# A rotary embedding over 16 heads: the first piece of the first tile loaded in two halves of 64 partitions, ahead of the tables

## The chip, the cores and the metric

The kernel runs on one core of a Trainium2 chip. The metric is the device time of one execution in microseconds; the time given for a kernel is the median of its runs. A core has five engines (TensorE, VectorE, ScalarE, GpSimd, SyncE) with a queue of instructions each, and 16 DMA engines that move the data. A DMA is issued by an instruction on an engine's queue (here SyncE's and ScalarE's), and its packets then wait in a ring that belongs to that queue, one on each DMA engine.

## The reference

```
batch, seq, dim = x.shape            # 16, 512, 1024, float32
x = x.reshape(batch, seq, 16, 64)    # 16 heads of 64
x1, x2 = x[..., :32], x[..., 32:]
cos, sin: (512, 32), the same for every batch and head
out = concatenate([x1 * cos - x2 * sin, x1 * sin + x2 * cos], axis=-1)
```

Every element is read once and written once: 33.6 MB in and 33.6 MB out.

## The kernel before

**Tiles.** One tile holds two batches: 128 partitions, 64 for each batch (PB), and on each partition KK = 8 consecutive rows of 1024 elements, 32 KB. There are NT = 8 tiles of 4 MB and BUFS = 5 buffers for them, so tiles 0 to 4 are loaded at once and tiles 5 to 7 when the stores of tiles 0 to 2 have landed. Tiles are changed in place and stored from the same buffer.

**Loads and stores.** `load` (L70) and `store` (L76) each issue one DMA for the rows lo to hi of a tile. Before the change the order is this: SyncE issues the sin table (L83, 64 partitions of 1 KB), ScalarE the first piece of tile 0, rows 0 to 2 (L84; FIRST = (3, 8)), SyncE the cos table (L85), ScalarE the second piece, rows 3 to 7 (L87), and SyncE tiles 1 to 4 (L89). Then SyncE issues four tiny DMAs, `spare` (L92; EXTRA gives their numbers of rows). Stores are issued by SyncE, a whole tile at a time, only the last tile in two pieces of four rows (LAST_OUT, L193). After the third store SyncE issues the loads of tiles 5 to 7 (L198).

**Semaphores of the DMAs.** All DMAs that are issued by SyncE and ScalarE share eight semaphores in turn, in program order. So the ninth DMA waits, before it is issued, for the first to land, and so on: the spares wait for the tables and the pieces of tile 0, and the stores of tiles 0 to 2 wait for earlier loads too.

**Tables.** sin and cos arrive on 64 partitions. TensorE spreads them to 128 by a matrix of zeros and ones (`spread`), sin at L113 and cos at L114, both into one PSUM tile `tab`. VectorE then makes the signed sin table `sns` in SBUF (L116, L117) and a copy for row 0 (L119). L116 is released by TensorE's last matmul at L114. Everything else waits for these.

**Arithmetic of one tile.** The order is written out by hand (`manual_schedule`). GpSimd multiplies the swapped rows by `sns` (`sin_product`, L165): rows 1 and 2, then row 3, rows 4 and 5, rows 6 and 7. VectorE multiplies by cos into PSUM (`cos_product`, L141) and adds the two for the row pairs (`pair_sum`, L189). For row 0 (L150) and row 3, TensorE adds by a matmul with the identity (`pe_add`, L176) and ScalarE copies the sum back (L209, L181). The first work of GpSimd on a tile needs rows 1 and 2; VectorE's needs row 0; row 3 comes second on GpSimd.

**The end.** The last tile's first store (rows 0 to 3) waits for ScalarE's last copy at L181; its second store for VectorE's last sum at L189. The execution ends when the second store has landed.

Of the kernel before, what the change touches and what calls it, by code (L numbers as in the profile page):

```python
# [21 lines left out]
FIRST = (3, 8)  # L22
LAST_OUT = (4, 8)

EXTRA = (2, 4, 5, 6)


@with_exitstack
def kernel(
# [13 lines left out]
    nc = tc.nc  # L43
    P = nc.NUM_PARTITIONS
# [4 lines left out]
    PB = P // NB  # L49
    KK = seq // PB  # L50
# [3 lines left out]
    x_v = x.rearrange("(t b) (p k) d -> t (b p) (k d)", b=NB, k=KK)  # L54
# [12 lines left out]

    tiles = [None] * NT

    def load(t, lo=0, hi=KK, queue=nc.sync):  # L70
        if tiles[t] is None:
            tiles[t] = xp.tile([P, F], FP32, name="xt")
        s = slice(lo * dim, hi * dim)
        queue.dma_start(out=tiles[t][:, s], in_=x_v[t][:, s])

    def store(t, lo=0, hi=KK):  # L76
        s = slice(lo * dim, hi * dim)
        nc.sync.dma_start(out=out_v[t][:, s], in_=tiles[t][:, s])

    tabs = bp.tile([P, 2 * dim], FP32, name="b")  # L80
    sin_sb = tabs[:PB, : KK * half]
    cos_sb = tabs[:PB, dim : dim + KK * half]
    nc.sync.dma_start(out=sin_sb, in_=sin_v)  # L83
    load(0, 0, FIRST[0], nc.scalar)  # L84
    nc.sync.dma_start(out=cos_sb, in_=cos_v)  # L85
    for lo, hi in zip(FIRST, FIRST[1:]):
        load(0, lo, hi, nc.scalar)  # L87
    for t in range(1, BUFS):
        load(t)  # L89
    spare = fixed.tile([16, len(EXTRA), 16], FP32)  # L90
    for i, n in enumerate(EXTRA):
        nc.sync.dma_start(out=spare[:n, i], in_=sin_v[:n, :16])  # L92
# [7 lines left out]
    for ps in (own_ps[:, :BANK], own_ps[:, BANK:], pe_ps):  # L100
# [9 lines left out]
        out=spread.rearrange("p (b q) -> p b q", b=NB),  # L110
        in_=bass.AP(tensor=eye.tensor, offset=eye.offset, ap=[eye.ap[0], [0, NB], [1, PB]]),
# [147 lines left out]
```

## Time and profile before

| | |
|---|---|
| median of 3 runs | 163.85 us (163.66 to 164.0) |
| the profiled execution's own time | 163.66 us |
| its span | 161.9 us, 443 instructions |
| VectorE, GpSimd busy | 136.2 us, 127.1 us |
| bytes moved by the DMAs | 67.25 MB, 415 GB/s over the span |
| first piece of tile 0 issued, SyncE's first DMA issued | 0.73 us, 0.73 us |
| table matmuls begin: sin, cos | 8.13 us, 12.26 us |
| GpSimd's first product begins | 14.36 us |
| last tile's first and second store issued | 149.85 us, 152.0 us |

The page gives busy times by engine, the DMA queues (q1 is SyncE's, q10 ScalarE's) with their share of the 16 DMA engines' time, and a chain of waits followed back from the last instruction. Stretches of the span can be asked for by themselves: each line then gives a window in us, its length, the busy time of TensorE, its weight loads, VectorE, ScalarE and GpSimd with counts, the granted clock, the share of the 16 DMA engines' time, and GB/s. A DMA share a little over 1 comes from packets that are counted where they begin. Besides, the trace keeps a record of each DMA packet: queue, begin, length and bytes. A packet here is the run of one partition, so a piece of three rows gives 128 packets of 12 KB, eight for each of the 16 DMA engines; a record does not name its engine, but each engine handles one packet after the other, so begins and ends chain up into 16 lanes.

### The profile page before, as it was taken

What the parts mean: (1) busy time and instruction counts of PE and PEld (TensorE: products, weight loads), DVE (VectorE), ACT (ScalarE), POOL (GpSimd) and SP (SyncE); (2) the same over time, 40 slices, a digit from 0 to 9 for tenths busy, and PEclk for the clock granted to TensorE, in tenths of its full rate; (3) what the DMA queues carried; (4) which work ended last, traced back from release to release, by engine and by line L of the source; (5) the groups of instructions that cost most, each with busy time, mean ns of one, the idle gap of its engine ahead of it and who ended that gap; (6) DMA issues with size and microseconds to landing.
All of it is one profiled execution on the core that took longest, in us unless ns stands there. A gap on an engine that the chain in (4) does not pass through costs nothing.

```text
span 161.9 us, 443 instructions
## 1 busy us (share of the span) xinstructions
PE 61.2 (38%) x71; PEld 19.1 (12%) x71; DVE 136.2 (84%) x85; ACT 18.7 (12%) x25; POOL 127.1 (79%) x38
## 2 busy tenths in 40 slices
PE   3023290507550575039311923093407540574000
PEld 0011130102110211012101310040003100210000
DVE  1006996999999999999999999999999999999500
ACT  0000231100310030102010121003100310031000
POOL 1004999999999999998899889988998999891000
PEclk9999999555865577555855595558555765567555
DMA  5999999999999999998999999999998998996796
GB/s 182 432 398 445 429 478 389 429 478 389 429 478 389 405 502 389 405 502 389 421 480 389 437 470 389 437 470 389 429 478 389 445 462 389 470 429 275 328 449 259
DMA packets 2787, 67.25 MB, mean 415 GB/s; under 512 B 354, under 2 KB 482, under 8 KB 482
## 3 DMA queue, kind: packets, MB, share of 16 engines
q1 hardware_dynamic: 2498, 63.05, 90.6%
q10 hardware_dynamic: 288, 4.19, 6.7%
q14 instruction: 1, 0.01, 0.0%
HBM read 33.69 MB, written 33.55 MB: 415 GB/s over the span
## 4 chain that ended last, share of the span: by engine, by line
DVE 68%; issue 13%; DMA 7%; POOL 5%; PE 1%; SPq 0%; DVEq 0%
DVE xt L189 33%; DVE pd L141 31%; DMA b<-in_cos_dram 7%; POOL b L165 5%; DVE pe_ps L141 3%; PE tab L114 1%; SPq L83 0%; DVE sns L116 0%; DVE xt L150 0%; DVE own_ps L141 0%; DVE sns L117 0%; DVEq L189 0%
## 5 line engine op out<-in xcount | busy, mean ns | idle before, releaser
L165 POOL TENSOR_TENSOR b<-xt,sns 128x2048 f32<-128x2048 f32 (+1 forms) x32 | 126.4, 3982 | 18.5 <-DVE sns L117 13.1
L189 DVE TENSOR_TENSOR xt<-pd,b 128x2048 f32<-128x2048 f32 x24 | 54.9, 2286 | 2.4 <-POOL b L165 1.6
L141 DVE TENSOR_TENSOR pd<-xt,tab 128x2048 f32<-128x2048 f32 x24 | 55.0, 2291 | 0.2
L176 PE MATMUL own_ps<-xt,ident 128*128 128x512 f32 x32 | 30.2, 1100 | 54.4 <-DVE xt L150 48.7
L176 PE MATMUL pe_ps<-b,ident 128*128 128x512 f32 x32 | 28.8, 1001 | 23.9 <-DVE pe_ps L141 23.9
L176 PEld LDWEIGHTS own_ps<-xt,ident 128*128 128x128 f32 x32 | 9.4, 324 | 74.4 <-DVE xt L150 59.7
L209 ACT COPY xt<-own_ps 128x1024 f32<-128x1024 f32 x8 | 8.1, 1012 | 73.7 <-PE own_ps L176 73.7
L181 ACT COPY xt<-pe_ps 128x512 f32<-128x512 f32 x16 | 9.4, 585 | 38.2 <-PE pe_ps L176 38.2
L176 PEld LDWEIGHTS pe_ps<-b,ident 128*128 128x128 f32 x32 | 8.4, 289 | 42.8 <-DVE pe_ps L141 34.1
L141 DVE TENSOR_TENSOR pe_ps<-xt,tab 128x512 f32<-128x512 f32 x16 | 11.0, 686 | 0.0
L116 DVE TENSOR_SCALAR sns<-tab 128x256 f32<-128x256 f32 x1 | 0.4, 424 | 12.0 <-PE tab L114 12.0
L141 DVE TENSOR_TENSOR own_ps<-xt,tab 128x1024 f32<-128x1024 f32 x8 | 9.8, 1224 | 0.0
L150 DVE TENSOR_TENSOR xt<-xt,tab 128x1024 f32<-128x1024 f32 x8 | 9.7, 1214 | 0.0
L209 ACT ACT_TABLE_LOAD x1 | 1.3, 1283 | 19.2 <-DVE xt L150 19.2
L113 PE MATMUL tab<-b,spread 64*128 64x256 f32 x2 | 1.2, 698 | 5.5 <-DMA b<-in_sin_dram 5.5
L114 PE MATMUL tab<-b,spread 64*128 64x256 f32 x2 | 1.2, 712 | 2.9 <-DMA b<-in_cos_dram 2.9
L101 PE MATMUL own_ps<-zero 128*128 128x512 bf16 x2 | 1.0, 622 | 1.2 <-DVE zero L97 1.2
L113 PEld LDWEIGHTS tab<-b,spread 64*128 64x128 f32 x2 | 0.5, 310 | 6.4 <-issue 6.4
L97 DVE MEMSET zero<- 128x256 uint32 x1 | 0.3, 272 | 0.9 <-PEq L240 0.9
L114 PEld LDWEIGHTS tab<-b,spread 64*128 64x128 f32 x2 | 0.5, 308 | 3.7 <-DMA b<-in_cos_dram 3.7
L101 PE MATMUL pe_ps<-zero 128*128 128x512 bf16 x1 | 0.6, 634 | 0.0
L101 PEld LDWEIGHTS <-zero 128*128 128x128 bf16 x3 | 0.3, 125 | 1.5 <-DVE zero L97 1.2
(9 smaller groups left out, 1.8 us busy)
## 6 DMA issues: line engine op xcount, KB each, us to landing
xt<-in_x_dram SPq DMA_DIRECT2D x7, 4096.0 KB, 35.1
out_dram<-xt SPq DMA_DIRECT2D x7, 4096.0 KB, 20.8
out_dram<-xt SPq DMA_DIRECT2D x2, 2048.0 KB, 7.7
xt<-in_x_dram ACTq DMA_DIRECT2D x1, 2560.0 KB, 15.0
xt<-in_x_dram ACTq DMA_DIRECT2D x1, 1536.0 KB
b<-in_sin_dram SPq DMA_DIRECT2D x1, 64.0 KB
b<-in_cos_dram SPq DMA_DIRECT2D x1, 64.0 KB
spare<-in_sin_dram SPq DMA_DIRECT2D x1, 0.1 KB
```

Source lines behind the costliest of these rows:

```text
L97: nc.vector.memset(zero, 0.0)
L101: nc.tensor.matmul(out=ps, lhsT=zero[:, :P], rhs=zero, start=True, stop=True)
L113: nc.tensor.matmul(out=sin_t, lhsT=spread, rhs=sin_sb, start=True, stop=True)
L114: nc.tensor.matmul(out=cos_t, lhsT=spread, rhs=cos_sb, start=True, stop=True)
L116: nc.vector.tensor_scalar_mul(out=sns[:, :, 0, :], in0=sin_k, scalar1=-1.0)
L141: nc.vector.tensor_tensor(out=o, in0=i, in1=cb, op=ALU.mult)
L150: nc.vector.tensor_tensor(out=heads(r), in0=heads(r), in1=s, op=ALU.mult)
L165: nc.gpsimd.tensor_tensor(out=o, in0=i, in1=sb, op=ALU.mult)
L176: nc.tensor.matmul(out=ps, lhsT=ident, rhs=other, start=False, stop=True, skip_group_check=True)
L181: nc.scalar.copy(out=r, in_=pe_ps)
L189: nc.vector.tensor_tensor(out=r, in0=ps, in1=b, op=ALU.add)
L209: nc.scalar.copy(out=r0, in_=own_ps)
```

## The change

The first piece of tile 0 becomes two DMAs, partitions 0 to 63 from SyncE and 64 to 127 from ScalarE, both the first DMA of their queue. SyncE then issues sin, cos and the second piece of tile 0, which was ScalarE's, and tiles 1 to 4 as before. One of the four spares goes, so that twelve DMAs still stand ahead of the first store. The stores are the same; the last tile was stored in two pieces before and still is.

```diff
-EXTRA = (2, 4, 5, 6)
+EXTRA = (2, 4, 5)
...
-    def load(t, lo=0, hi=KK, queue=nc.sync):
+    def load(t, lo=0, hi=KK, shares=((nc.sync, 0, P),)):
         if tiles[t] is None:
             tiles[t] = xp.tile([P, F], FP32, name="xt")
         s = slice(lo * dim, hi * dim)
-        queue.dma_start(out=tiles[t][:, s], in_=x_v[t][:, s])
+        for queue, a, b in shares:
+            queue.dma_start(out=tiles[t][a:b, s], in_=x_v[t][a:b, s])
...
+    load(0, 0, FIRST[0], ((nc.sync, 0, PB), (nc.scalar, PB, P)))
     tabs = bp.tile([P, 2 * dim], FP32, name="b")
     sin_sb = tabs[:PB, : KK * half]
     cos_sb = tabs[:PB, dim : dim + KK * half]
     nc.sync.dma_start(out=sin_sb, in_=sin_v)
-    load(0, 0, FIRST[0], nc.scalar)
     nc.sync.dma_start(out=cos_sb, in_=cos_v)
     for lo, hi in zip(FIRST, FIRST[1:]):
-        load(0, lo, hi, nc.scalar)
+        load(0, lo, hi)
     for t in range(1, BUFS):
         load(t)
```

The order of the instructions on TensorE, VectorE and GpSimd is the same before and after. In the new order the fourth whole-tile load (tile 4) is the ninth DMA, so it waits for SyncE's half of the first piece to land before it is issued, and the three spares stand behind it.

## The prediction

> **What bounds the kernel now.** I read the page's engine table first, then the DMA queues, then the stretches around both ends.
>
> ```profile
> span 161.9 us, 443 instructions
> ...
> PE 61.2 (38%) x71; PEld 19.1 (12%) x71; DVE 136.2 (84%) x85; ACT 18.7 (12%) x25; POOL 127.1 (79%) x38
> ...
> DMA  5999999999999999998999999999998998996796
> ...
> q1 hardware_dynamic: 2498, 63.05, 90.6%
> q10 hardware_dynamic: 288, 4.19, 6.7%
> ```
>
> The busiest engine has 84%, the 16 DMA engines 90.6 + 6.7 = 97.3%. The transfers bound this kernel; only the first and the last few slices have room. The chain of waits names VectorE for 68% of the span, but VectorE is merely busy without a break between the two ends. So I cut the ends into stretches (the last two columns are the DMA share and GB/s):
>
> ```profile
> 2.70:6.20 3.50, 0.00 (x0) 0.00 (x0) 0.00 (x0) 0.00 (x0) 0.00 (x0) 1.00 0.96 401
> ...
> 7.80:11.30 3.50, 1.19 (x2) 0.50 (x2) 0.00 (x0) 0.00 (x0) 0.00 (x0) 1.00 1.01 399
> 11.30:13.30 2.00, 1.04 (x2) 0.50 (x2) 0.00 (x0) 0.00 (x0) 0.00 (x0) 1.00 1.02 436
> ...
> 16.00:146.00 130.00, 55.59 (x62) 17.51 (x62) 127.45 (x76) 18.16 (x24) 124.59 (x32) 0.63 1.00 431
> ```
>
> ```profile
> 147.00:148.00 1.00, 0.55 (x1) 0.30 (x2) 1.00 (x2) 0.00 (x0) 0.00 (x0) 0.91 1.06 459
> 148.00:149.00 1.00, 1.00 (x2) 0.00 (x0) 1.00 (x1) 0.00 (x0) 0.00 (x0) 0.50 0.16 66
> 149.00:150.00 1.00, 0.21 (x1) 0.00 (x0) 0.90 (x2) 0.58 (x1) 0.00 (x0) 0.50 0.08 33
> 150.00:151.00 1.00, 0.00 (x0) 0.00 (x0) 1.00 (x1) 0.00 (x0) 0.00 (x0) 0.50 0.62 262
> ```
>
> The transfers run without a hole from 2.7 to 148 us. Then nearly all engines idle for about 2 us, because the last tile's first store is not issued before 149.85 (SyncE waits for the last ScalarE copy, L181). That hole is the only place where earlier arithmetic buys time. Where the arithmetic starts is shown by the chain in order of time (start, length):
>
> ```profile
> 1.34 10.88 DMA b<-in_cos_dram
> 12.22 0.04 issue
> 12.26 1.23 PE tab L114 x2
> 13.49 0.02 issue
> 13.52 0.42 DVE sns L116
> 13.94 0.34 DVE sns L117
> 14.28 0.07 issue
> 14.36 1.89 POOL b L165
> ```
>
> All arithmetic waits for cos, 64 KB that take 10.88 us to land. The trace's packet records tell why: cos's four 1 KB packets per DMA engine alternate one for one with ScalarE's 20 KB packets (0.82 us each).
>
> **The change, part by part.** The span ends when the last transfer lands, so the sum has two terms: G, what closes of the hole and of the alternation, and L, what the first piece costs more in two halves.
>
> *Tables behind the first piece.* First, arithmetic. The first piece is eight 12 KB packets per DMA engine (0.460 us each) whichever queues carry it; before, the last ended at 6.58 with up to three sin packets (0.046) among them, so about 6.45 alone. Sin and cos follow on SyncE's ring, 2 x 4 x 0.046 = 0.37, so cos lands near 6.85 + L. SyncE issues half, sin, cos, rest in turn, 0.55 us each by its rows at L83 and L85, so cos is issued near 1.9: early enough. From sin's semaphore to its matmul 0.6 us, 1.19 us of sin matmuls, then cos's 1.23: L116 starts near 9.65 + L instead of 13.52. The arithmetic is early by 3.9 - L. Nothing takes that back: row 3 is first read 4.5 us after GpSimd's start (18.82 against 14.36), so at 15.0 + L, and the rest of tile 0, eight 20 KB packets of 0.762 behind cos, lands near 13.1 + L; tile 1 is read near 27 and lands near 23 + L. L delays the arithmetic and the stream of transfers alike, so 3.9 us of lead close a hole of 2 us whatever L is.
>
> Now G. By the packet records, 15 of 16 engines end tile 6's store between 148.66 and 149.38 and one at 150.44; all begin the last tile at 150.68 to 150.83; the last ends at 160.69. Without a hole each goes on for 16 packets of 0.615, 9.85 us: 149.38 gives 159.23, a gain of 1.46; the late engine gives 160.29, a gain of 0.40. (Two of its packets took 1.83 and 1.88 us, not 1.21; I can't tell whether that recurs.) Also, 20 KB packets beside cos packets took a median of 0.819 and without one 0.762: 4 x 0.057, and 0.1 on the first 20 KB packet, 0.33 in all, goes. G is 0.40 + 0.33 = 0.7 to 1.46 + 0.33 = 1.8; I take 1.2, between a lone late engine and none.
>
> *Two halves of 64 partitions.* No row shows a large transfer into 64 partitions; the nearest are the tables, which go to 64 partitions beside 128-partition packets. Lower bound: beside sin, the 12 KB packets kept their 0.460, so a 64-partition packet costs its own time and L = 0 (below that only the 0.14 of sin packets, counted already). Upper bound: in cos's stage each 0.046 packet stretched its neighbour by 0.057, on all 16 engines, so it cost 0.103, 2.24 times its own time; the stretch 7.8 to 11.3 above shows it as a DMA share of 1.01 at 399 GB/s, against 436 right after. The first packet is a cold wait of about 1.2 us either way, so seven packets count: 7 x 0.460 x 1.24 = 4.0. Between them: the 20 KB packet right after sin took 0.85 to 0.88, 0.107 above 0.762, or 0.027 for each of four sin packets, a factor of 1.58. I take 1.75, near this row because its packets stand beside 12 KB ones as here, a little above because now every packet goes to 64 partitions: L = 7 x 0.460 x 0.75 = 2.4.
>
> [...]
>
> *The queues.* ScalarE issues one DMA instead of two, SyncE one more in front and one spare fewer. The twelve DMAs ahead of the first store stay twelve. The fourth whole-tile load now waits for SyncE's half to land (near 6.5 + L instead of being issued by 4.2), with three spares behind it; its packets have their turn near 42, so I cost it at nothing. The dropped spare is six packets of 64 bytes: nothing. TensorE, VectorE, GpSimd keep their order.
>
> **Sum:** L - G = 2.4 - 1.2 = +1.2 us on the profiled execution's 163.66 (its span 161.87, and 1.79 around it). The median of the runs is 0.19 above it, so I add to 163.85: **165.0**. With L from 1.6 to 3.6 that case runs from 164.2 to 166.3.
>
> **Rivals.**
> - *Halves cost nothing* (L near 0). Then only G is left: -0.7 to -1.8, about 162.6. For it: 12 KB packets at exactly 0.460 beside sin's. Against: the stretched packets in cos's stage. The place is the seven packets, and it decides where a packet into 64 partitions costs under 1.27 times its time (L under 1.2 - 0.33). 0.35. This includes a half late on SyncE: sin's first packet began 4.4 us after its issue (0.73 to 5.13) where ScalarE's began after 1.0; if SyncE's half does so, the engines run dry from about 4.3 to 5.1, L = 0.8, 163.4.
> - *The terms cancel* (L within 0.33 of G): the early cos is paid for by the halves, 163.9. 0.12.
> - *Halves cost as in cos's stage or more*: L = 4.0, +2.2 to +3.3, about 166.6. 0.13.
>
> **How the numbers follow.** Mine has 0.40. Slower by over 0.2% (0.33 us, about what a measurement here can tell) is 0.40 + 0.13 = 0.53, faster 0.35, same 0.12. The range leaves out the lowest end of the first rival and the upper half of the last: 161.9 to 166.5.
>
> **What would show it.** In the packet records, the first piece's 12 KB packets above 0.460: near 0.8 supports me, 0.46 the first rival. The first table matmul near 9.6 (7.2 + L) and GpSimd's first product near 12.9 (10.5 + L). In the stretches, first 10 us below 401 GB/s if L is real; no hole near 149 in any case. If the hole is still there, my slack is wrong; if the tables land early and the whole DMA stream is not late, L is wrong.

## The result, and the profile after

The changed kernel takes 165.97 us (165.94 to 166.02, four runs) against 163.75 us of the kernel before in the same session: a ratio of 1.0136, 95% interval 1.0119 to 1.0154. It is slower by 2.2 us. The profiled execution took 166.02 us, its span is 164.2 us. In the code after the change the lines lie one further down (L142 for L141, and so on).

The stretches of the changed kernel, columns as before the change (window, length, TensorE, weight loads, VectorE, ScalarE, GpSimd, clock, DMA share, GB/s):

```profile
2.70:6.20 3.50, 0.00 (x0) 0.00 (x0) 0.00 (x0) 0.00 (x0) 0.00 (x0) 1.00 0.99 225
6.20:10.00 3.80, 0.00 (x0) 0.00 (x0) 0.00 (x0) 0.00 (x0) 0.00 (x0) 1.00 1.03 226
...
11.00:16.00 5.00, 2.04 (x4) 1.17 (x4) 2.65 (x5) 0.00 (x0) 1.87 (x1) 1.00 1.04 446
16.00:146.00 130.00, 55.56 (x62) 17.21 (x62) 127.45 (x76) 18.18 (x24) 124.58 (x32) 0.63 1.00 432
```

The first line is the same window that moved 401 GB/s before. The DMA engines are as busy (0.99) and move 225 GB/s: they are occupied and slow, not idle. This goes on to 10 us, as long as the two halves last; from 11 us on the rate is the old one. The packet records say it packet by packet. SyncE's 12 KB packets took a median of 0.947 us and ScalarE's 0.907, where the whole piece had 0.460; the two queues were not served "at once" but nearly one after the other (SyncE's from 2.09 to 6.28 us, ScalarE's from 5.09 to 9.94), and all 16 engines took part in both. So the first piece ends at 9.94 us.

The other end of the same kernel:

```profile
147.00:148.00 1.00, 0.78 (x2) 0.30 (x2) 1.00 (x2) 0.00 (x0) 0.00 (x0) 0.86 1.21 524
148.00:149.00 1.00, 0.84 (x1) 0.00 (x0) 1.00 (x1) 0.12 (x1) 0.00 (x0) 0.50 1.14 492
149.00:150.00 1.00, 0.00 (x0) 0.00 (x0) 0.90 (x2) 0.47 (x1) 0.00 (x0) 0.50 0.91 393
150.00:151.00 1.00, 0.00 (x0) 0.00 (x0) 1.00 (x1) 0.00 (x0) 0.00 (x0) 0.50 0.76 328
```

The hole at 148 to 150 us is gone. The last tile's first store was issued at 149.49, hardly earlier than before (149.85), but now the stream of transfers is the late one: tile 6's store ends between 151.90 and 153.33, and the last packet at 163.06 instead of 160.69.

The chain in order of time (start, length, what):

```profile
1.34 9.73 DMA b<-in_sin_dram
11.07 0.14 issue
11.21 1.19 PE tab L114 x2
12.40 0.87 PE tab L115 x2
13.26 0.02 issue
13.29 0.42 DVE sns L117
13.71 0.34 DVE sns L118
14.05 0.07 issue
14.13 3.15 POOL b L166
```

cos no longer waits behind 20 KB packets; sin and cos come together (their packets begin from 7.65 to 10.28 us), behind the first piece. But they come as late as the first piece ends, and GpSimd starts at 14.13, 0.23 us earlier than before.

### The profile page after: what moved, and what is told of

Read it like the earlier page. It is cut to its first block, busy times and chain, and to the rows that moved or that the text cites. A ratio compares the mean times of both kernels' runs of the same rounds, so it can differ in the third digit from the quotient of the medians.

```text
span 164.2 us, 445 instructions
## 1 busy us (share of the span) xinstructions
PE 60.7 (37%) x71; PEld 19.0 (12%) x71; DVE 136.2 (83%) x85; ACT 18.8 (11%) x25; POOL 127.2 (77%) x38
## 4 chain that ended last, share of the span: by engine, by line
DVE 67%; issue 12%; POOL 6%; DMA 6%; PE 1%; SPq 0%; DVEq 0%
DVE xt L190 32%; DVE pd L142 30%; POOL b L166 6%; DMA b<-in_sin_dram 6%; DVE pe_ps L142 3%; PE tab L114 1%; PE tab L115 1%; SPq L75 0%; DVE sns L117 0%; DVE own_ps L142 0%; DVE xt L151 0%; DVE sns L118 0%; DVEq L190 0%
## 5 line engine op out<-in xcount | busy, mean ns | idle before, releaser
L142 DVE TENSOR_TENSOR pd<-xt,tab 128x2048 f32<-128x2048 f32 x24 | 55.0, 2291 | 0.2
L142 DVE TENSOR_TENSOR pe_ps<-xt,tab 128x512 f32<-128x512 f32 x16 | 11.0, 685 | 0.0
L142 DVE TENSOR_TENSOR own_ps<-xt,tab 128x1024 f32<-128x1024 f32 x8 | 9.8, 1223 | 0.0
## 6 DMA issues: line engine op xcount, KB each, us to landing
out_dram<-xt SPq DMA_DIRECT2D x2, 2048.0 KB, 10.3
xt<-in_x_dram SPq DMA_DIRECT2D x1, 2560.0 KB, 14.6
```

Of the source, the lines that this page charges most:

```text
L142: nc.vector.tensor_tensor(out=o, in0=i, in1=cb, op=ALU.mult)
```

## The experiments

The theory: the first piece in two halves of 64 partitions costs L = 3.5 us in the stream of transfers, since only partitions of one half are written at a time; the tables' new place gives G = 1.3. Each experiment is the changed kernel with the edit shown, unless it says otherwise; `...` marks lines left out. The rivals, one by one: the tables' place itself costs; two queues at the start cost; the source of a half (one batch) costs; it belongs to the cold start.

### The whole piece (e1) and its cut by columns (e2)

```diff
-EXTRA = (2, 4, 5)
+EXTRA = (2, 4, 5, 6)
...
-    load(0, 0, FIRST[0], ((nc.sync, 0, PB), (nc.scalar, PB, P)))
+    load(0, 0, FIRST[0])
```

> The first piece as one DMA of 128 partitions, first on SyncE, tables behind it; four spares again. Theory (a transfer into 64 partitions at a time runs at half rate, L = 3.5 of the measured +2.2, G = 1.3): L goes, 12 KB packets back at 0.46 us, cos matmul begins near 8.4, no hole near 149, time 1.0 to 1.8 us below the kernel before, near 162.3. Rival (putting the tables behind the first piece, on SyncE's ring, is itself the cost): near 166 like the change.

Measured: 162.56 us, ratio to the kernel before 0.9924 (0.9909 to 0.9939). The first piece's packets are back at 0.467 us and end at 6.46, the first table matmul begins at 7.71 and cos's at 8.70, GpSimd at 10.63. This kernel beats both. Against the kernel before it has the tables behind the first piece, and both pieces of tile 0 on SyncE's queue with them; together that is worth 1.33 us (163.89 to 162.56 in the same session). Against the change it has the halves undone and one spare more, 3.4 us.

```profile
2.70:6.20 3.50, 0.00 (x0) 0.00 (x0) 0.00 (x0) 0.00 (x0) 0.00 (x0) 1.00 0.94 389
...
148.00:149.00 1.00, 0.00 (x0) 0.00 (x0) 0.27 (x1) 0.00 (x0) 0.00 (x0) 0.50 0.62 262
149.00:150.00 1.00, 0.00 (x0) 0.00 (x0) 0.00 (x0) 0.00 (x0) 0.00 (x0) 0.50 1.00 426
```

These are e1's stretches: 389 GB/s at the start, and no hole at 149 us (VectorE is already done at 148.3). GpSimd's first product in e1 (start, length, engine, line, operation):

```profile
10.63 4.51 POOL L166 TENSOR_TENSOR b<-xt,sns 128x2048 f32<-128x2048 f32 x1 [9.33 <-DVE sns L118]
```

The packet records show L in the stream itself. The first 20 MB have been moved by 49.31 us in e1 and by 52.83 in the change, 60 MB by 141.85 and 145.31, and the last packet ends at 159.57 and 163.06: the change is 3.5 us late from the start to the end.

For e2 the piece stays split over both queues, but by columns, 6 KB packets to all 128 partitions:

```diff
-    load(0, 0, FIRST[0], ((nc.sync, 0, PB), (nc.scalar, PB, P)))
...
+    mid = FIRST[0] * dim // 2
+    for queue, c in ((nc.sync, 0), (nc.scalar, mid)):
+        queue.dma_start(out=tiles[0][:, c : c + mid], in_=x_v[0][:, c : c + mid])
```

> The first piece in two DMAs from SyncE and ScalarE at once as in the change, but split by columns: each goes to all 128 partitions with packets of 6 KB. Theory (64 partitions): packets at 0.23 us, the first piece done near 6.5 to 6.7, time near 162.3 as with one DMA. Rival (two queues at once at the start are the cost: one ring is served after the other): first piece done near 9.9 as in the change, time near 166.

Measured: 162.57 us, 0.9917 (0.9902 to 0.9931); packets 0.23 us, the piece done at 6.48. Splitting over two queues costs nothing, and gains nothing over e1. e2 has the queues and the three spares of the change and differs from it in the direction of the cut alone, so the cut at partition 64 is what costs the 3.4 us.

### Another source (e3), one queue (e4)

```diff
-    load(0, 0, FIRST[0], ((nc.sync, 0, PB), (nc.scalar, PB, P)))
...
+    n = FIRST[0] * dim
+    x_m = x_v[0].rearrange("(q e) c -> e q c", e=2)
+    for queue, e in ((nc.sync, 0), (nc.scalar, 1)):
+        queue.dma_start(out=tiles[0][e * PB : (e + 1) * PB, :n], in_=x_m[e][:, :n])
```

> The change, but each half's 64 partitions are filled from every second row of the piece, so from both batches (4 MB of HBM instead of 2 MB); the rows of tile 0's first piece thereby stand on other partitions than the reference has them. Theory (the 64 partitions written are the cost): packets stay at 0.95 us, time near 166.0. Rival (reading 64 neighbouring rows of one batch is the cost): packets at 0.46 us, time near 162.3.

Measured: 165.93 us, 1.0124 (1.0108 to 1.0140), packets 0.959 and 0.907 us. Every second row of two batches went as slowly as 64 neighbouring rows of one in the change (165.97 us, 0.947 and 0.907), so the place that is read is not the cost. (e3 puts rows on other partitions and so computes something else than the reference; only its time is of use.)

```diff
-    load(0, 0, FIRST[0], ((nc.sync, 0, PB), (nc.scalar, PB, P)))
+    load(0, 0, FIRST[0], ((nc.sync, 0, PB), (nc.sync, PB, P)))
```

> The same two halves, both issued by SyncE one after the other. Theory (64 partitions; in the change one half is served after the other already): the same as the change, 166.0 within 0.5. Rival (the two queues get in each other's way): faster than the change by 1 us or more.

Measured: 166.13 us, 1.0139 (1.0123 to 1.0155), packets 0.939 us, the piece done at 9.94 as in the change. Two queues "at once" (the change, 165.97 us) were no better and no worse than two DMAs in turn on one.

### The halves in the kernel before (e5)

```diff
-    load(0, 0, FIRST[0], nc.scalar)
...
+    n = FIRST[0] * dim
+    for a, b in ((0, PB), (PB, P)):
+        nc.scalar.dma_start(out=tiles[0][a:b, :n], in_=x_v[0][a:b, :n])
```

> The halves alone: the kernel before with its tables ahead, and the first piece as two DMAs of 64 partitions, both issued by ScalarE (one spare fewer). Theory (halves cost L = 3.5 in the stream of transfers, and cos still waits behind ScalarE's packets, so the arithmetic is late as well and the hole stays): slower by about 3 to 3.5 us, near 167. Rival (the hole of 2 us near 149 absorbs most of a late start): slower by 1.5 us, near 165.3.

Measured: 176.76 us, 1.0799 (1.0777 to 1.0822). Both expectations missed (this experiment is an edit of the kernel before). GpSimd's waits in e5:

```profile
POOL b L169 <- DMA xt<-in_x_dram: 26.6, 2, 15.4
```

GpSimd waited twice for tile 0, first for the first piece, then 11.2 us for row 3. In the kernel before, ScalarE's first packets came at 1.74 us, and SyncE's ring got its first turn only at 5.13; SyncE was still busy with the tables' small packets, until 10.94, while ScalarE's pieces went through. In e5 the tables' packets came first (2.06 against 2.34 us) and were out of the way at 6.7, so that from 7.8 us on SyncE's 32 KB packets of tile 1 alternated with ScalarE's pieces of tile 0. The first piece was done at about 14.6 us, the second at 30.6. So e5 undid the order of the queues along with the halves, and its time tells nothing of L. It does point at what the old arrangement leaned on: who is served first.

### The tables beside the first piece (e6)

```diff
-    nc.sync.dma_start(out=sin_sb, in_=sin_v)
+    nc.scalar.dma_start(out=sin_sb, in_=sin_v)
-    nc.sync.dma_start(out=cos_sb, in_=cos_v)
+    nc.scalar.dma_start(out=cos_sb, in_=cos_v)
```

(on e1)

> The first piece whole on SyncE as in e1, the tables on ScalarE's queue beside it instead of behind it. Theory (with the hole closed the stream of transfers alone sets the end): same as e1, 162.5 within 0.4, wherever the arithmetic starts. Rival (the arithmetic still counts): the time moves with GpSimd's first product, by more than 0.5 us.

Measured: 163.65 us, 0.9993 (0.9976 to 1.0011): as slow as the kernel before, 1.1 us above e1. My expectation was wrong and the rival right. From a queue of their own the tables' 1 KB packets alternate again with 20 KB packets, the cos matmul begins at 12.01 and GpSimd at 14.11, and the hole is back:

```profile
147.00:148.00 1.00, 0.77 (x1) 0.50 (x2) 1.00 (x2) 0.00 (x0) 0.00 (x0) 0.50 1.21 524
148.00:149.00 1.00, 1.00 (x2) 0.00 (x0) 1.00 (x1) 0.00 (x0) 0.00 (x0) 0.50 0.08 33
149.00:150.00 1.00, 0.31 (x1) 0.00 (x0) 0.90 (x2) 0.59 (x1) 0.00 (x0) 0.50 0.00 0
150.00:151.00 1.00, 0.00 (x0) 0.00 (x0) 1.00 (x1) 0.00 (x0) 0.00 (x0) 0.50 0.61 262
```

GpSimd's first product in e6 begins 3.5 us later than in e1:

```profile
14.11 22.57 POOL L166 TENSOR_TENSOR b<-xt,sns 128x2048 f32<-128x2048 f32 x6 [12.80 <-DVE sns L118]
```

I had taken "the hole is closed" for granted where it had to be earned by early tables. This is the cleanest evidence for G: the same loads with the tables on another queue, arithmetic at 14.11 instead of 10.63, and about 1.1 us lost. The alternation came back too, but it is not where the time goes: by the packet records the first 60 MB have been moved by 141.99 us in e6, 141.85 in e1 and 141.93 in the kernel before. The three part only after that, at the hole.

### A tile in the middle (e7, e9, e10)

```diff
-        load(t)
+        load(t, 0, KK, ((nc.sync, 0, PB), (nc.sync, PB, P)) if t == 2 else ((nc.sync, 0, P),))
```

(on e1)

> e1 with tile 2, in the middle of the stream, loaded as two halves of 64 partitions from SyncE (one spare fewer). Theory (any transfer into partitions 0 to 63 or 64 to 127 alone runs at half rate): 32 KB packets at 2.43 us instead of 1.21, the tile 9.7 us longer, time 9.7 above e1, near 172.2; arithmetic has slack for most of it. Rival (the half rate belongs to the cold start): near 162.5.

Measured: 172.87 us, 1.0564 (1.0545 to 1.0583), 10.3 above e1. Tile 2's packets took a median of 2.57 us (1.218 in e1), so the half rate is no matter of the start. For e9 the list of parts is `((nc.sync, 32, 96), (nc.sync, 0, 32), (nc.sync, 96, P))`:

> As e7, but tile 2 is cut as partitions 32 to 95, 0 to 31, 96 to 127, one DMA after the other from SyncE (two spares). e7 gave 2.57 us for each 32 KB packet into one half. Theory (what counts is whether partitions under 64 and over 63 are both written at once): the four packets per engine into 32 to 95 take 1.21 us, those into the two quarters 2.57, so the tile costs half of e7's 10.3 more than e1, near 167.7. Rival (a transfer of 64 partitions is slow whichever they are): 2.57 throughout, near 172.9.

Measured: 167.63 us, 1.0270 (1.0204 to 1.0336). The first line is the stretch in which e9 loads partitions 32 to 95 of tile 2, the second the two quarters:

```profile
22.50:27.30 4.80, 2.08 (x2) 0.50 (x2) 4.80 (x4) 0.33 (x1) 4.80 (x2) 0.65 1.00 430
27.40:38.50 11.10, 4.67 (x6) 1.74 (x6) 11.06 (x7) 1.01 (x2) 11.10 (x4) 0.54 0.99 227
```

and the first of these windows in e7, where it loads partitions 0 to 63:

```profile
22.50:27.30 4.80, 2.07 (x2) 0.50 (x2) 4.80 (x4) 0.35 (x1) 4.80 (x2) 0.68 1.13 246
```

Every packet into 32 to 95 took 1.213 us, the time of a full tile's packet; those into the two quarters took a median of 2.49. 64 partitions as such were not slow (1.213 us); 64 partitions on one side of partition 64 were (2.57 us in e7). (The profiled execution of e9 was its slowest, 169.5 us: there the packets after tile 2, from 39 to 59 us, took 1.36 us, which I can't explain. Tile 2 itself lies before that.) In e10 the list has four quarters of 32 in rising order:

> As e7, but tile 2 in four quarters of 32 partitions in rising order from SyncE (one spare), each 1 MB with two 32 KB packets per engine. Theory (32 partitions reach no fewer sides than 64 of one half): packets at 2.57 us and the time of e7, 172.9. Rival (the rate falls with the number of partitions): packets near 5 us, the tile about 20 us longer still, 185 to 195.

Measured: 173.14 us, 1.0582 (1.0538 to 1.0626), packets 2.57 us: 32 partitions of one side went at the same rate as 64 of it (2.57 us in e7).

### The first piece cut through the middle (e8)

```diff
-    load(0, 0, FIRST[0], ((nc.sync, 0, PB), (nc.scalar, PB, P)))
+    load(0, 0, FIRST[0], ((nc.sync, 32, 96), (nc.scalar, 0, 32), (nc.scalar, 96, P)))
```

> The change with another cut: SyncE loads partitions 32 to 95 of the first piece, ScalarE 0 to 31 and 96 to 127 (two spares). [...] Rival (a transfer of 64 partitions is slow whichever they are): all 12 KB packets at 0.95, time near 166.

Measured: 164.03 us, 1.0030 (1.0010 to 1.0049), the piece done at 8.29. By the ratios to the kernel before (1.0136 for the change) that is 1.7 us below the change, half of L = 3.5, and the rival's 166 did not come. The packets do not show why: ScalarE's ran from 1.74 and SyncE's from 3.17 us, interleaved, and took 0.73 and 0.83 us, where the whole piece had 0.46 and the change's halves 0.95. Only e9, on one queue, shows the two kinds apart.

## Why the prediction was right, point by point

- *What bounds it.* Right. The DMA engines had no hole but the one near 149, and everything that happened is read from the stream of transfers. (One engine had ended tile 6's store at 148.56, not 148.66; nothing was worked out from that end.)
- *Tables behind the first piece, G = 1.2.* The size is right: e1 has this part without the halves and gains 1.33 us by the medians, 1.12 by the last packet of the profiled executions (160.69 to 159.57). Its make-up is not. The prediction added 0.33 for the alternation that goes, to about 0.87 for the hole. No gain from the alternation shows: at 60 MB the kernel before (141.93) is level with e1 (141.85), and in e1 each engine's first 20 KB packet, right behind the tables, took a median of 1.12 us instead of 0.762, which is about what the alternation had cost. So G is the hole alone, worth more than the prediction gave it, and that the two errors cancel is luck. The late engine is in e1 too (it ends tile 6's store at 149.85, the rest by 149.34), which is why the gain is less than the hole.
- *Two halves, L = 2.4.* Right in kind, too small. L is 3.5: the first piece ended at 9.94 instead of 6.46, and 165.97 - 163.75 + 1.33 = 3.55. The term that was mis-sized is the factor of 1.75 for a packet into 64 partitions: it is 0.947 / 0.460 = 2.06, and seven packets at that factor give 3.4. I chose 1.75 near sin's row because its packets stood beside 12 KB ones, but that row (1.58) misled; the longer stage with cos (2.24) was the better witness, and the middle between them (1.91) would have given 2.9. The measured +2.2 lies in the range, near its upper end, because the range took in L up to 3.6.
- *Why two queues did not help.* Two halves on two queues (the change, 165.97 us) were no better than two in turn on one (e4, 166.13). I had drawn both rings as served in turn. In the change SyncE's four packets per engine nearly all went first, so that the 16 engines wrote the same half at the same time: at 3.5 and at 5.0 us all 16 packets under way were SyncE's. One packet of 12288 bytes in 0.947 us on each of 16 engines makes 208 GB/s. What halves that are served truly in turn would have cost, no run shows.
- *Rivals.* Halves that cost nothing: refuted by e2 against the change. SyncE's half late: no, it was first (from 2.09 us, ScalarE's from 5.09). Terms that cancel: no. Halves that cost as in cos's stage (L = 4.0, +2.2 to +3.3): its L was nearer to the measured 3.5 than mine, and +2.2 is where its span begins; I gave it 0.13, too little.
- *What would show it.* No hole near 149 came as said. The first table matmul was said for 9.6 and GpSimd's first product for 12.9; they came at 11.21 and 14.13, since the measured L puts them at 10.7 and 14.0. The 0.5 us that is left at the matmul stands in e1 too (7.71 where the same working gives 7.2), so the step from the tables' arrival to the matmul was read too short; the two table matmuls then took 2.05 us together instead of the 2.42 added up, and GpSimd was on time again.

Not settled: what in the chip makes one side slow. The runs show which 32 KB packets were slow (a median of 2.57 us in e7 and e10, 2.49 into e9's quarters) and which were not (1.213 us into e9's 32 to 95, 1.218 in e1); the trace does not show the cause.

## What to carry to other kernels

Let a DMA that loads a tile write partitions on both sides of 64. Here, splitting one at partition 64 doubled the time of its packets, on two queues or on one at the start (0.947 and 0.939 us against 0.460) and in the middle (2.57 us against 1.218), while a split by columns was free (e2, 162.57 us against e1's 162.56). Stores were not tried. Put small transfers that release the arithmetic on the same ring behind the piece they are needed with: there the tables' last packet ended at 6.81 us (e1), and on a ring of their own, in turn with large packets, at 10.66 (e6). Where the transfers bound a kernel, look for the hole in their stream first: earlier arithmetic was worth 1.1 to 1.3 us here, less than that hole.

## What the runs showed of the hardware

- In e9 a 64-partition slice from 32 to 95 ran at the rate of a whole tile (1.213 us for each 32 KB packet, 430 GB/s; 1.218 us in e1), in e7 one from 0 to 63 at half of it (2.57 us).
- At the start, the change's halves of 64 partitions took SyncE and ScalarE 0.55 us each to issue, and in e4 the first packets came 1.34 us after the issue began (2.07 against 0.73). The whole piece into 128 partitions took 0.38 us and 1.02 us (e1). I can't say why.
- 32 KB packets into 32 partitions of one side took the same 2.57 us as into 64 of it (e10, e7).
- Two rings were not served in turn from the start: in the kernel before about six of ScalarE's packets went through on each engine before SyncE's first (5.13 us against 1.74, both issued at 0.73), in the change SyncE's four before nearly all of ScalarE's (from 2.09 and from 5.09). Later they took turns: in the kernel before cos's 1 KB packets came between 20 KB ones until 10.94 us.
